# Second float32r part of each weight: ScalarE's negated first part and an adding transfer, in place of VectorE's difference

## The chip, the core and the metric

The kernel runs on one core of one Trainium2 chip. The metric is the device time of one execution in microseconds (us); three runs of the kernel before have a median of 1448.61 us (1447.63 to 1450.83).

## What is computed

One decoder layer on 512 tokens of width 1024, in float32: a SwiGLU feed-forward network (FFN 1), a token mixer that runs gated linear attention (GLA) and softmax attention with forget gates (FoX) side by side and merges them, and a second feed-forward network (FFN 2). Every sub-layer has an RMSNorm before and after it, and shift, scale and gate from a conditioning vector.

```python
h = rmsnorm(x, g_pre[0]) * (1 + sc1) + sh1
x = x + 0.5 * gt1 * rmsnorm(swiglu(h, w_gu1, w_dn1), g_post[0])
h = rmsnorm(x, g_pre[1]) * (1 + sc2) + sh2
x = x + gt2 * rmsnorm(token_mixer(h, ...), g_post[1])
h = rmsnorm(x, g_pre[2]) * (1 + sc3) + sh3
x = x + 0.5 * gt3 * rmsnorm(swiglu(h, w_gu2, w_dn2), g_post[2])
```

All weights are float32: w_gu1 and w_gu2 are 1024 x 5632, w_dn1 and w_dn2 2816 x 1024, w_in 1024 x 8224, w_pa, w_pb and w_out 1024 x 1024, and w_ada, which makes shift, scale and gate, 1024 x 9216.

## The kernel before

**Two parts of every operand.** TensorE takes float32r operands, which have fewer bits than float32. So each weight and each activation is held as two float32r tiles: a first part `hi` (the value rounded) and a second part `lo` (the value minus `hi`). A product is three matmuls, hi by hi, hi by lo and lo by hi (`PARTS`, line 188; `mm3`, line 190). Two of the three read the weight's `hi`, one reads its `lo`.

**Weights come in chunks.** `Block` (line 159) cuts a weight matrix into chunks of 128 x 1024 values (512 KB). `raw_load` (line 147) allocates one of four raw buffers (`NRAW = 4`, tag `raw`) and SyncE issues the load into it. `split` (line 152) allocates one of five `whi` and one of five `wlo` buffers (`NW = 5`); ScalarE copies the raw chunk, rounded, into `whi` (line 155), and VectorE writes raw minus `whi` into `wlo` (line 156). There are 220 chunks; 218 of their differences run on VectorE, two on GpSimd by the argument `eng` (both in the first block, behind the calls of lines 497 and 506). Each chunk feeds 24 matmuls of 512 columns, in whichever stage it is used.

**A ring of buffers.** A raw buffer is free for the next load when both parts have been made; a `whi` or `wlo` buffer is free when the last matmul that reads it is done. `ada_acc` (line 202) loads parts of w_ada into the same four raw buffers, where VectorE multiplies them up (lines 211 and 213), and `two_parts` (line 216) puts the result's two parts into a `wlo` buffer.

**Stages.** The first FFN's first column block is written out by hand, interleaved with the first modulation (from line 444 on, its order fixed by `in_order`). `ffn` (line 381) then runs eleven blocks of gate and up columns, four chunks each, and `down` (line 408) the second matrix in two halves of the output columns, one chunk for two rows of 128, except the last six rows of the second half. Beside the first chunks of a first half, `down` calls `mod_gate` (line 279) twice: it loads four raw buffers of w_ada, sums them on VectorE, splits the sum (`two_parts`) and has TensorE add it over the partitions (lines 294 and 295). The mixer stages take their projections as steps of `Fill`, whose loads are asked for four steps ahead (`LOOK = 4`), with FoX and then GLA work between the steps.

**Order.** Outside the parts fixed by hand, a planner orders the instructions of each engine from the program order and its own estimate of when each is ready. Loads are moved ahead as far as buffers allow, and the matmuls of one product can be moved apart. On the chip each engine then runs its list strictly in that order, and waits at an instruction whose inputs are late.

Of the kernel before, what the change touches and what calls it, by code (L numbers as in the profile page):

```python
# [8 lines left out]
F32 = mybir.dt.float32  # L9
# [3 lines left out]
AF = mybir.ActivationFunctionType  # L13
ALU = mybir.AluOpType
# [25 lines left out]
def tile_hybrid_layer(  # L40
# [4 lines left out]
    nc = tc.nc  # L45
# [12 lines left out]
    def nm(s):  # L58
        uid[0] += 1
        return f"{s}_{uid[0]}"  # L60
# [4 lines left out]
    def tmp(shape=(P, 512), dt=F32):  # L65
        return sb.tile(list(shape), dt, tag="t2", bufs=NTMP, name=nm("t2"))
# [17 lines left out]
    @contextmanager  # L84
    def in_order(last):

        start = len(nc.cur_bb.bb.instructions)
        yield
        for i in list(nc.cur_bb.bb.instructions)[start:]:
            if i.engine in last:  # L90
                after_inst(i, last[i.engine])
            last[i.engine] = i
# [44 lines left out]
    def small_columns():  # L137
        rps = aux((P, P))
        nc.tensor.transpose(rps[:, :108], rows[:108, :], ident[:108, :108])
        nc.vector.tensor_copy(cols, rps[:, :108])  # L140
        cth = small(8)
        nc.scalar.activation(cth, cols[:, 96:104], AF.Tanh, scale=0.5)
        nc.vector.scalar_tensor_tensor(csil, cth, 1.0, cols[:, 96:104], ALU.add, ALU.mult)
        nc.vector.tensor_scalar(csil, csil, 0.5, None, ALU.mult)
# [7 lines left out]
    def split(raw, shape, eng=None):  # L152
        hi = sb.tile([P] + list(shape), F32R, tag="whi", bufs=NW, name=nm("whi"))
        lo = sb.tile([P] + list(shape), F32R, tag="wlo", bufs=NW, name=nm("wlo"))
        nc.scalar.copy(hi, raw)  # L155
        (eng or nc.vector).tensor_tensor(lo, raw, hi.bitcast(F32), ALU.subtract)  # L156
        return hi, lo

    class Block:
# [17 lines left out]
        def load(self, a=0, b=None, eng=None):  # L177
            self.fetch(a, b)
            for r, n in self.spans(a, b):
                if self.parts[r] is None:  # L180
                    hi, lo = split(self.raw[r], (n, self.args[4]), eng)
                    for j in range(n):
                        self.parts[r + j] = (hi[:, j, :], lo[:, j, :])
# [13 lines left out]
    def hilo(hi, lo, src, eng=None):  # L197
        nc.scalar.copy(hi, src)  # L198
        (eng or nc.vector).tensor_tensor(lo, src, hi.bitcast(F32), ALU.subtract)  # L199
# [21 lines left out]
    def ada_fetch_first(ch):  # L221

        w2 = w_ada[:, 0:2 * D].rearrange("(k p) (m c) -> p k m c", p=P, m=2)
        us = []
        for k in range(KD):
            u = unit()
            nc.sync.dma_start(u.rearrange("p (m c) -> p m c", m=2), w2[:, k, :, ch * 256:(ch + 1) * 256])
            us.append(u)
        return us

    def ada_sum_a(us, ks):

        for k in ks:
            nc.scalar.activation(us[k], us[k], AF.Copy, scale=csil[:, k:k + 1])
            if k:
                nc.gpsimd.tensor_tensor(us[0], us[0], us[k], ALU.add)

    def ada_sum_b(us, k0):

        a = tmp()  # L240
        nc.vector.tensor_scalar(a, us[k0], csil[:, k0:k0 + 1], None, ALU.mult)
        for k in range(k0 + 1, KD):
            nc.vector.scalar_tensor_tensor(a, us[k], csil[:, k:k + 1], a, ALU.mult, ALU.add)
        nc.vector.tensor_tensor(a, a, us[0], ALU.add)
        return a
# [19 lines left out]
    def mod_reduce(a):  # L265
        ps = aux((P, 4))
        for j in range(4):
            nc.tensor.matmul(ps[:, j:j + 1], a[:, j * P:(j + 1) * P], ones[:, 0:1], start=True, stop=True)  # L268
        return ps

    def mod_turn(shc, scc, i, ch, ps):
        js = slice(2 * ch, 2 * ch + 2)
        b0 = 24 * i + 2 * ch
        g0 = 72 + 8 * i + 2 * ch
        nc.vector.scalar_tensor_tensor(scc[:, js], ps[:, 2:4], 1.0, cols[:, b0 + 8:b0 + 10], ALU.add, ALU.add)
        nc.vector.tensor_tensor(shc[:, js], ps[:, 0:2], cols[:, b0:b0 + 2], ALU.add)
        nc.vector.tensor_tensor(scc[:, js], scc[:, js], cols[:, g0:g0 + 2], ALU.mult)
# [41 lines left out]
    def x_stat(t):  # L319
        ss = small(2)  # L320
        for h in range(2):
            sumsq(xt[t][h], ss[:, h:h + 1])
        return rstd_of(ss[:, 0:1], ss[:, 1:2], D)
# [9 lines left out]
    def x_turned(tp, xn, dp, bank=aux):  # L333

        ps = bank((P, 2, 256))
        for j in range(2):
            d = 2 * dp + j
            for e in range(2):
                nc.tensor.transpose(ps[:, j, e * P:(e + 1) * P], xn[e][d // 4][:, (d % 4) * P:(d % 4 + 1) * P], ident)
        return ps  # L340
# [27 lines left out]
    def gu_blocks(w_gu, jb):  # L368
        return Block(w_gu, 0, KD, jb * 256, 256), Block(w_gu, 0, KD, DFF + jb * 256, 256)

    def gu_matmuls(ps, gw, uw, hs, ks, ts, js=range(4), late=False):

        for j in js:
            cs = slice(j // 2 * P, (j // 2 + 1) * P)
            p_, w_ = ps[j // 2][j % 2], (gw, uw)[j % 2]
            for n, (k, i, e) in enumerate([(k, *ie) for k in ks for ie in PARTS] if not late else
                                          [(k, *ie) for ie in ((0, 0), (1, 0), (0, 1)) for k in ks]):
                nc.tensor.matmul(p_[:, ts], w_[k][i][:, cs], hs[k][e][:, ts],  # L378
                                 start=ks[0] == 0 and n == 0, stop=ks[-1] == KD - 1 and n == 3 * len(ks) - 1)
# [61 lines left out]
    first = gu_blocks(w_gu1[0], 0)  # L441
    ps0 = [[acc(), acc()] for _ in range(2)]
    last = {}
    with in_order(last):
        ada = []
        for ch in range(4):
            ada.append(ada_fetch_first(ch))
            if ch % 2 == 0:
                for b in first:
                    b.fetch(2 * ch, 2 * ch + 4)  # L450
        rs_ = []
        xn = []

        def norm(t):

            xx = sb.tile([P, D], F32, tag="wlo", bufs=NW, name=nm("xn"))
            for h in range(2):
                nc.vector.tensor_scalar(xx[:, h * 512:(h + 1) * 512], xt[t][h], rs_[t], None, ALU.mult)
            xn.append([xx[:, 0:512], xx[:, 512:1024]])

        for t in range(NT):
            rs_.append(x_stat(t))
            if t == 1:
                norm(0)
                small_columns()

        def turn(tp, dp, eng):
            ps = x_turned(tp, xn[2 * tp:2 * tp + 2], dp, (aux, acc)[dp % 2])
            for j in range(2):
                eng(xT[2 * dp + j][:, tp * 256:(tp + 1) * 256], ps[:, j])  # L470

        def modulated(ch, a, n):

            mod_turn(sh1, sc1, 0, ch, mod_reduce(a))
            ht = [tmp() for _ in range(2)]
            for e in range(2):
                d = 2 * ch + e
                nc.vector.tensor_scalar(ht[e], xT[d], sc1[:, d:d + 1], sh1[:, d:d + 1], ALU.mult, ALU.add)
            if ch < 3:
                ada_sum_a(ada[ch + 1], range(n))  # L480
            for e in range(2):
                d = 2 * ch + e
                hilo(hs[d][0], hs[d][1], ht[e])
            if ch < 3:
                ada_sum_a(ada[ch + 1], range(n, ROWS_A[ch + 1]))

        norm(1)
        norm(2)
        for dp in range(4):
            turn(0, dp, nc.vector.tensor_copy)  # L490
            if dp == 0:
                norm(3)
        ada_sum_a(ada[0], range(ROWS_A[0]))
        for dp in range(4):
            turn(1, dp, nc.scalar.copy)
        a = ada_sum_b(ada[0], ROWS_A[0])
        first[0].load(0, 4)
        first[1].load(0, 4, nc.gpsimd)
        modulated(0, a, 3)
        for ch in range(4):  # L500
            ks, part = (2 * ch, 2 * ch + 1), 3 if ch < 3 else 4
            gu_matmuls(ps0, *first, hs, ks, slice(0, 512), range(part), True)
            if ch < 3:
                a = ada_sum_b(ada[ch + 1], ROWS_A[ch + 1])
                if ch == 1:
                    first[0].load(4, 8)
                    first[1].load(4, 8, nc.gpsimd)
                modulated(ch + 1, a, (5, 4, 0)[ch])
            gu_matmuls(ps0, *first, hs, ks, slice(0, 512), range(part, 4), True)
# [647 lines left out]
```

## Time and profile before

| | before |
|---|---|
| median of 3 runs | 1448.61 us |
| profiled execution | 1448.71 us |
| its span, first to last instruction | 1447.0 us |
| TensorE (PE) busy | 1398.0 us, 97% |
| VectorE (DVE) busy | 764.7 us, 53% |
| ScalarE (ACT) busy | 531.6 us, 37% |
| GpSimd (POOL) busy | 207.3 us, 14% |
| mean busy share of the 16 DMA engines | 39% |
| mean granted TensorE clock | 0.996 |

Stages by the span's time: first block and first modulation to about 65 us, FFN 1's gate and up blocks to about 293, its second matrix to about 430, mixer to about 1062, FFN 2 to the end, with its second matrix from about 1315. In the rows, an engine's name with a q (SPq) is the queue of the engine; "xN" is a number of instructions; in a timeline the bracket tells how long the engine sat idle ahead of the row and what ended that wait. Matmuls overlap in the rows: what counts is the distance between their starts.

### The profile page before, as it was taken

The page shows a single profiled execution, that of the slowest core. Times are in us where ns is not written, and L with a number is a line of the kernel's source. Part 1 is how long each engine was busy: PE and PEld are TensorE (multiplying, and loading weights), DVE is VectorE, ACT ScalarE, POOL GpSimd, SP SyncE. Part 2 cuts the span into 40 slices and gives each one's busy share as a digit, 9 for nine tenths or more (in the row PEclk, how much of TensorE's full clock was granted, in tenths as well). Part 3 has the DMA queues.
Part 4 walks back from the last instruction along what each step waited for, and adds up shares of the span by engine and source line. Part 5 has one row for each costly group of instructions (what it writes and reads, how often), then busy time and mean ns, then how long its engine had stood idle before and what let it go on. Part 6 is the DMA issues. An engine that isn't in the chain of part 4 may idle for free.

```text
span 1447.0 us, 17080 instructions
## 1 busy us (share of the span) xinstructions
PE 1398.0 (97%) x6477; PEld 1123.6 (78%) x6477; DVE 764.7 (53%) x1210; ACT 531.6 (37%) x915; POOL 207.3 (14%) x328
## 2 busy tenths in 40 slices
PE   5899999999999999999999999999999999999998
PEld 4688888878877877777888887788888888887886
DVE  6945544272266689762645546538464434337232
ACT  6332322232244376663733334332353322222221
POOL 6200000000041544340110212100050000000001
PEclk9999999999999999999999999999999999999999
DMA  9544543272335755322332222126613233235411
GB/s 322 158 147 146 155 150 101 60 247 93 96 120 161 227 160 175 95 69 79 97 109 73 73 73 59 59 72 182 197 45 117 87 102 99 91 87 188 132 59 59
DMA packets 160623, 174.40 MB, mean 121 GB/s; under 512 B 8842, under 2 KB 127734, under 8 KB 160540
## 3 DMA queue, kind: packets, MB, share of 16 engines
q1 hardware_dynamic: 160540, 173.31, 39.1%
q8 instruction: 51, 0.84, 0.2%
q14 instruction: 32, 0.26, 0.1%
HBM read 169.05 MB, written 4.23 MB: 120 GB/s over the span
## 4 chain that ended last, share of the span: by engine, by line
PE 83%; DVE 9%; ACT 2%; issue 2%; POOL 1%; DMA 1%; SPq 0%; DVEq 0%; POOLq 0%; ACTq 0%
PE mm L192 44%; PE mm L378 33%; DVE wlo L156 1%; PE aux L980 1%; DVE t L213 1%; PE mm L802 1%; DMA raw<-in_w_dn_dram 1%; PE aux L791 1%; DVE u L779 1%; ACT jk L314 1%; PE aux L268 1%; POOL sm L310 1%; ACT u L775 0%; DVE u L199 0%; DVE u L766 0%
## 5 line engine op out<-in xcount | busy, mean ns | idle before, releaser
L156 DVE TENSOR_TENSOR wlo<-raw,whi 128x1024 fp32r<-128x1024 f32 x218 | 272.3, 1252 | 404.4 <-ACT whi L155 395.2
L378 PE MATMUL mm<-u,whi 128*128 128x512 f32 (+1 forms) x1472 | 451.8, 390 | 10.1 <-ACT u L198 9.7
L155 ACT CAST whi<-raw 128x1024 fp32r<-128x1024 f32 x220 | 230.1, 1050 | 542.3 <-PE mm L192 300.1
L192 PE MATMUL mm<-whi,u 128*128 128x512 f32 x1216 | 390.2, 397 | 1.5 <-ACT u L198 1.5
L378 PEld LDWEIGHTS mm<-u,whi 128*128 128x128 f32 x1472 | 274.7, 190 | 75.4 <-ACT u L198 12.9
L192 PE MATMUL mm<-u,whi 128*128 128x512 f32 x896 | 289.3, 401 | 0.8 <-DVE u L1007 0.8
L378 PE MATMUL mm<-u,wlo 128*128 128x512 f32 (+1 forms) x736 | 283.1, 388 | 0.0
L192 PEld LDWEIGHTS mm<-whi,u 128*128 128x128 f32 x1216 | 228.2, 188 | 54.2 <-ACT u L198 1.7
L192 PE MATMUL mm<-wlo,u 128*128 128x512 f32 x608 | 240.2, 395 | 0.0
L192 PEld LDWEIGHTS mm<-u,whi 128*128 128x128 f32 x896 | 166.9, 189 | 39.2 <-DVE u L1007 1.2
L192 PE MATMUL mm<-u,wlo 128*128 128x512 f32 x448 | 178.4, 399 | 0.0
L378 PEld LDWEIGHTS mm<-u,wlo 128*128 128x128 f32 x736 | 139.6, 190 | 30.9
L192 PEld LDWEIGHTS mm<-wlo,u 128*128 128x128 f32 x608 | 114.2, 188 | 28.0
L192 PEld LDWEIGHTS mm<-u,wlo 128*128 128x128 f32 x448 | 84.7, 189 | 19.6
L307 POOL TENSOR_SCALAR sm<-ss 128x1 f32<-128x1 f32 x12 | 2.3, 191 | 667.6 <-ACT jk L314 667.6
L198 ACT CAST u<-t 128x512 fp32r<-128x512 f32 (+1 forms) x84 | 44.5, 537 | 114.0 <-DVE t L401 78.4
L213 DVE SCALAR_TENSOR_TENSOR t<-raw,csil,t 128x512 f32<-128x512 f32 x98 | 74.0, 755 | 3.3 <-DMA raw<-in_w_ada_dram 1.1
L748 POOL TENSOR_SCALAR u<-t,Ft 128x128 f32<-128x128 f32 (+1 forms) x64 | 43.9, 695 | 89.8 <-DMA t<-Fd 77.7
L400 DVE SCALAR_TENSOR_TENSOR t<-t,mm 128x512 f32<-128x512 f32 x44 | 30.1, 684 | 47.0 <-ACT t L399 47.0
L399 ACT ACTIVATE t<-mm 128x512 f32<-128x512 f32 x44 | 26.1, 594 | 63.2 <-PE mm L378 63.2
L401 DVE SCALAR_TENSOR_TENSOR t<-t,mm 128x512 f32<-128x512 f32 x44 | 30.2, 687 | 30.8 <-PE mm L378 29.2
L199 DVE TENSOR_TENSOR u<-t,u 128x512 fp32r<-128x512 f32 x52 | 35.6, 689 | 16.1 <-ACT u L198 15.9
(178 smaller groups left out, 1121.3 us busy)
## 6 DMA issues: line engine op xcount, KB each, us to landing
raw<-in_w_gu_dram SPq DMA_DIRECT2D x88, 512.0 KB, 4.0
raw<-in_w_in_dram SPq DMA_DIRECT2D x64, 512.0 KB, 3.8
raw<-in_w_dn_dram SPq DMA_DIRECT2D x44, 512.0 KB, 3.7
raw<-in_w_ada_dram SPq DMA_DIRECT2D x64, 256.0 KB, 3.1
raw<-in_w_ada_dram SPq DMA_DIRECT2D x24, 512.0 KB, 3.9
u<-in_w_ada_dram SPq DMA_DIRECT2D x32, 256.0 KB, 6.5
raw<-in_w_in_dram SPq DMA_DIRECT2D x20, 256.0 KB, 3.1
t<-Fd SPq DMA_DIRECT2D x16, 256.0 KB, 4.7
```

The costliest lines, as they stand in the source:

```text
L155: nc.scalar.copy(hi, raw)
L156: (eng or nc.vector).tensor_tensor(lo, raw, hi.bitcast(F32), ALU.subtract)
L192: nc.tensor.matmul(ps, a[i], b[j], start=first and n == 0, stop=last and n == 2)
L198: nc.scalar.copy(hi, src)
L199: (eng or nc.vector).tensor_tensor(lo, src, hi.bitcast(F32), ALU.subtract)
L213: nc.vector.scalar_tensor_tensor(a, raw[:, j, :], csil[:, k:k + 1], a, ALU.mult, ALU.add)
L268: nc.tensor.matmul(ps[:, j:j + 1], a[:, j * P:(j + 1) * P], ones[:, 0:1], start=True, stop=True)
L378: nc.tensor.matmul(p_[:, ts], w_[k][i][:, cs], hs[k][e][:, ts], start=ks[0] == 0 and n == 0, stop=ks[-1] == KD - 1 and n == 3 * len(ks) - 1)
L399: nc.scalar.activation(th, pg, AF.Tanh, scale=0.5)
L400: nc.vector.scalar_tensor_tensor(th, th, 1.0, pg, ALU.add, ALU.mult)
L401: nc.vector.scalar_tensor_tensor(th, th, 0.5, pu, ALU.mult, ALU.mult)
L748: nc.gpsimd.tensor_scalar(s_at(s, i), fb[:, 0:n], -1.0, Ft[:, i, h:h + 1], ALU.mult, ALU.add)
```

## The change

The new code in `split` is used wherever no engine is given. ScalarE runs a second instruction on the raw chunk, a copy with scale -1, into `wlo` (so it holds the first part with its sign turned), and GpSimd issues a transfer that reads the raw chunk and adds it, in float32, to what is in `wlo`. The raw buffer is then free when that transfer has read it, and the matmuls that read `wlo` wait for the transfer. Two calls in the first block now name VectorE and keep the old difference, so 216 of the 220 chunks go the new way, two stay on VectorE and two on GpSimd.

```diff
@@ split @@
         hi = sb.tile([P] + list(shape), F32R, tag="whi", bufs=NW, name=nm("whi"))
         lo = sb.tile([P] + list(shape), F32R, tag="wlo", bufs=NW, name=nm("wlo"))
         nc.scalar.copy(hi, raw)
-        (eng or nc.vector).tensor_tensor(lo, raw, hi.bitcast(F32), ALU.subtract)
+        if eng is None:
+
+            nc.scalar.activation(lo, raw, AF.Copy, scale=-1.0)
+            nc.gpsimd.dma_start(lo.bitcast(F32), raw, accum_op=ALU.add)
+        else:
+            eng.tensor_tensor(lo, raw, hi.bitcast(F32), ALU.subtract)
         return hi, lo
@@ first block @@
-        first[0].load(0, 4)
+        first[0].load(0, 4, nc.vector)
         first[1].load(0, 4, nc.gpsimd)
...
-                    first[0].load(4, 8)
+                    first[0].load(4, 8, nc.vector)
                     first[1].load(4, 8, nc.gpsimd)
```

## Rows read from the trace of the kernel before

**Rows 1.** The page: busy time of the engines, and the DMA queue of the loads.

```profile
PE 1398.0 (97%) x6477; PEld 1123.6 (78%) x6477; DVE 764.7 (53%) x1210; ACT 531.6 (37%) x915; POOL 207.3 (14%) x328
q1 hardware_dynamic: 160540, 173.31, 39.1%
```

**Rows 2.** The page's costliest groups, the two instructions of `split`: busy, mean ns, idle before.

```profile
L156 DVE TENSOR_TENSOR wlo<-raw,whi 128x1024 fp32r<-128x1024 f32 x218 | 272.3, 1252 | 404.4 <-ACT whi L155 395.2
L155 ACT CAST whi<-raw 128x1024 fp32r<-128x1024 f32 x220 | 230.1, 1050 | 542.3 <-PE mm L192 300.1
```

**Rows 3.** Timeline of ScalarE, then of VectorE, in FFN 1's second matrix.

```profile
323.85 1.05 ACT L155 CAST whi<-raw 128x1024 fp32r<-128x1024 f32 x1 [4.60 <-PE mm L192]
329.41 1.05 ACT L155 CAST whi<-raw 128x1024 fp32r<-128x1024 f32 x1 [4.51 <-PE mm L192]
...
324.93 1.23 DVE L156 TENSOR_TENSOR wlo<-raw,whi 128x1024 fp32r<-128x1024 f32 x1 [4.42 <-ACT whi L155]
```

**Rows 4.** Waits of SyncE's queue, in total, times, longest.

```profile
SPq L149 <- DVE wlo L156: 751.9, 154, 15.9
```

**Rows 5.** The page's DMA issues: KB each, median us from issue to landing.

```profile
raw<-in_w_dn_dram SPq DMA_DIRECT2D x44, 512.0 KB, 3.7
```

**Rows 6.** Groups by shape: two of GpSimd's instructions.

```profile
L236 POOL TENSOR_TENSOR u<-u,u 128x512 f32<-128x512 f32 x14 | 20.9, 1499 | 2.7 <-DMA u<-in_w_ada_dram 1.7 <-ACT u L234 0.3
L310 POOL TENSOR_TENSOR sm<-sm,mhalf 128x1 f32<-128x1 f32 x24 | 14.0, 584 | 2.0
```

**Rows 7.** Stretches: us, busy PE, PEld, DVE, ACT, POOL, PEclk, DMA share, GB/s.

```profile
110.00:290.00 180.00, 180.00 (x782) 145.26 (x782) 83.79 (x111) 48.16 (x60) 0.00 (x0) 1.00 0.41 123
290.00:330.00 40.00, 38.69 (x166) 30.82 (x166) 27.19 (x34) 12.09 (x14) 0.00 (x0) 1.00 0.70 237
330.00:420.00 90.00, 89.84 (x390) 72.18 (x388) 28.37 (x31) 24.65 (x41) 6.48 (x17) 1.00 0.30 97
1062.00:1320.00 258.00, 256.92 (x1198) 210.54 (x1199) 111.89 (x140) 76.93 (x110) 15.33 (x22) 1.00 0.31 94
1320.00:1345.00 25.00, 23.82 (x103) 18.87 (x102) 18.32 (x22) 7.84 (x9) 0.00 (x0) 1.00 0.85 285
```

**Rows 8.** Timeline where FFN 1's second matrix starts: SyncE, ScalarE, VectorE.

```profile
299.49 2.15 SPq L289 DMA_DIRECT2D raw<-in_w_ada_dram  x2
...
303.01 0.37 SPq L149 DMA_DIRECT2D raw<-in_w_dn_dram  x1
...
294.55 1.04 ACT L155 CAST whi<-raw 128x1024 fp32r<-128x1024 f32 x1
297.75 1.05 ACT L155 CAST whi<-raw 128x1024 fp32r<-128x1024 f32 x1 [2.15 <-DMA raw<-in_w_dn_dram]
...
307.84 1.05 ACT L155 CAST whi<-raw 128x1024 fp32r<-128x1024 f32 x1 [8.52 <-DMA raw<-in_w_dn_dram]
...
299.99 1.20 DVE L156 TENSOR_TENSOR wlo<-raw,whi 128x1024 fp32r<-128x1024 f32 x1
```

**Rows 9.** Timeline of TensorE in the same stretch.

```profile
298.47 1.33 PE L192 MATMUL mm<-whi,u 128*128 128x512 f32 x5
...
311.84 0.51 PE L294 MATMUL aux<-pair,ones 128*128 128x512 f32 x1 [1.31 <-ACT pair L198]
```

**Rows 10.** Timeline where FFN 1 leaves its first block: ScalarE, then VectorE.

```profile
59.02 2.00 ACT L155 CAST whi<-raw 128x1024 fp32r<-128x1024 f32 x2
...
60.10 2.36 DVE L156 TENSOR_TENSOR wlo<-raw,whi 128x1024 fp32r<-128x1024 f32 x2 [0.18 <-ACT whi L155]
```

**Rows 11.** The page's chain that ended last, by line; then a piece of it in FoX.

```profile
PE mm L192 44%; PE mm L378 33%; DVE wlo L156 1%; PE aux L980 1%; DVE t L213 1%; PE mm L802 1%; DMA raw<-in_w_dn_dram 1%; PE aux L791 1%; DVE u L779 1%; ACT jk L314 1%; PE aux L268 1%; POOL sm L310 1%; ACT u L775 0%; DVE u L199 0%; DVE u L766 0%
...
507.10 1.66 DVE wlo L156
```

**Rows 12.** Timeline of TensorE just behind that piece.

```profile
510.70 0.30 PE L762 MATMUL mm<-u,u 128*128 128x128 f32 x1 [1.31 <-DVE u L630]
```

**Rows 13.** Waits of the engines: one of GpSimd's, in total, times, longest.

```profile
POOL u L748 <- DMA t<-Fd: 77.7, 8, 34.9
```

## The prediction

> **What bounds the kernel now.** I read the busy times first. TensorE is busy 97% of the span, every other engine 53% or less [rows 1], so the end moves only where TensorE comes to wait, or stops waiting. The change touches no matmul. It takes a VectorE instruction out of the making of each weight chunk and puts a longer path in its place, so the question is how early a chunk is ready now. In FFN 1's second matrix ScalarE starts a first part every 5.56 us, each time after a wait for TensorE, that is, for one of the five `whi` buffers [rows 3]. One chunk's 24 matmuls thus take 5.6 us, 0.23 us each. A chunk begun when the fifth chunk ahead of it is done is needed four chunks later, after 4 x 5.6 = 22.4 us. Its second part is ready at 324.93 + 1.23 = 326.16, 2.3 us after 323.85 [rows 3], so it lies ready for 20 us. VectorE's difference is therefore hidden wherever the weights run ahead. It is not hidden where they have just begun to run: at the start of a second matrix [rows 8, 9] and at FFN 1's second column block [rows 10]. Last I read the DMA stretches [rows 7], because the change puts new work there.
>
> **VectorE loses** 216 x 1.252 us = 270 us [rows 2], from 765 to 494 us, off the path in most places. In the chain that ended last the difference stands with 1% of the span, 14 us [rows 11]. One of its pieces, 1.66 us in FoX, has a TensorE wait of 1.31 us for VectorE behind it [rows 11, 12]. What comes free there meets the next point.
>
> **ScalarE gains** 216 x 1.050 us = 227 us, taking the rounding copy as the row for the negated one [rows 2]: from 532 to 758 us, 52%. Each comes ahead of what ScalarE has queued next, in FoX the exponentials. At a place where VectorE gives 1.2 us back ScalarE takes 1.05. I put the whole middle at 0, with 6 us to either side (a gain above the 1.31 us [rows 12] at four or five such places, 14 us [rows 11] being all that the chain holds; a loss of the same count times 1.05).
>
> **GpSimd gains** 216 issues, an operation that the trace doesn't show from GpSimd. Bounds: SyncE's issue, 0.37 us [rows 8], and GpSimd's 512-column sum, 1.50 us [rows 6]. I take the row of GpSimd that moves next to nothing, 0.58 us [rows 6], as an issue moves no data itself: 126 us, from 14% to 23%. Behind a waiting issue stand GpSimd's norm and score instructions, which have room.
>
> **The adding transfer** isn't in the trace either. A load of 512 KB lands 3.7 us after its issue [rows 5]. In the stretch 330 to 420 the DMA engines were busy 0.30 x 90 = 27 us for 97 GB/s x 90 us = 8.73 MB, 16.65 chunks [rows 7]: 1.62 us of all engines for one chunk, and 2.1 us of the landing time for the rest. The adding transfer reads raw, reads `wlo` and writes `wlo`: between one pass (1.62) and three (4.86). I take two, 3.24 us, since the loads too read and write at once for their one pass. It then lands 2.1 + 3.24 = 5.3 us after its issue (3.7 to 7.0). The Trainium skill (Collectives: The Full Stack, "The bandwidth ceiling: the fold count and why AG ≠ RS ≠ AR") says that an add in the DMA engines costs two source reads for each chunk and nothing for the sum itself, which is my two passes; no run here shows it yet. Against that, its page DMA: Bandwidth & Descriptors ("Anatomy of one DMA — SWDGE (gpsimd) path") fits a transfer from GpSimd by 2.0 us and 436 GB/s, an estimate of 3.2 us here; by that the sum below would come to about 1455.
>
> **Second part, from the end of the first.** Before: 326.16 - 324.90 = 1.26 us [rows 3]. After: 1.05 + 0.58 + 5.3 = 6.93 us (5.1 to 9.6). It is 5.7 us later (3.9 to 8.3). Of the 20 us of lead 14 are left, 12 in the worse bound: in steady work this costs nothing, and the lead of three chunks is the cover.
>
> **The raw ring.** A raw buffer is now kept until the transfer is done, 5.7 us longer. SyncE's queue already waits 752 us for second parts ahead of weight loads [rows 4]. With the lead that too is free, except at the starts.
>
> **Start of a second matrix (two places).** At 301.2 VectorE ends a second part (299.99 + 1.20), and only then does SyncE issue the second of the two w_ada loads of its row (the row ends at 301.64); the next weight loads stand behind it, the first at 303.01 [rows 8]. After: the first part ends at 297.75 + 1.05 = 298.8, its second part at 305.7, 4.5 us later; the next weight load goes at 306.1, not 303.0, 3.1 us later, and the next first part starts at 310.9, not 307.84. The gate's sum is as late by 4.5 us, less two differences of 1.2 us that VectorE no longer does in between: its matmul, which already makes TensorE wait 1.31 us [rows 9], goes 2.1 us later, at 313.9. The 16 matmuls on the chunk's first part then run to 317.6; its second part is ready at 310.9 + 1.05 + 6.93 = 318.9: 1.3 us more. And the DMA engines are crowded: 0.70 x 40 = 28 us of loads plus 7 chunks (40 / 5.6) x 3.24 = 23 us make 51 us of work in 40, at FFN 2's 0.85 x 25 = 21 plus 4.5 x 3.24 = 15 make 36 in 25 [rows 7]. One load or adding transfer ahead in the line is 1.62 to 3.24 us; I add 2.5. Together 2.1 + 1.3 + 2.5 = 6 us, twice: **12 us** (0 to 24: none if the planner runs the first-part matmuls of several chunks ahead, as it does for five at 298.47 [rows 9]; 24 with the slower bounds).
>
> **First weights of FFN 1's second column block, and of FFN 2.** Two first parts from 59.02, two second parts by 62.46 [rows 10], needed from about 65. After: first parts end at 60.05 and 62.1, second parts come at 67.0 and 69.1. With the 2 x 16 first-part matmuls ahead (7.4 us) nothing waits, without it 2 us. I take 1 us each, **2 us** (0 to 8).
>
> **Sum.** 1448.7 (the profiled execution, 0.1 us above the median; its span with 1.7 us around it) + 12 + 2 + 0 = **1462.7 us, told as 1462**.
>
> **Rivals.** (1) The DMA engines run full. Now 39.1% x 1447 = 566 us [rows 1]; with 216 x 3.24 = 700 us, 87%. In 110 to 290 us, 0.41 x 180 = 74 us and 32 chunks x 3.24 = 104 make 178 of 180 [rows 7]: my own value lies at the edge, and above 3.3 us a transfer it decides. At 3.9 us this stretch is 19 us too long, and the starts take some 8 more than in my sum: 1490. At 4.86 the stretch needs 230 us (50 more), 1062 to 1320 needs 80 + 46 x 4.86 = 304 for 258 (46 more): about 1560. For it: two reads and a write are a bulk that the loads don't have. Against it: the rows written are 4 KB, the loads' half that or less. (2) VectorE's relief wins: the middle gives its full 6 us and first-part matmuls cover the starts: 1443. It decides if the starts cost under 3 us. For it: rows 11 and 12, and the five matmuls run ahead. Against it: ScalarE takes back nearly the same in the same place. (3) All of it hidden, both terms near zero: 1449. (4) A transfer stuck in GpSimd's queue behind an instruction that waits; GpSimd waits up to 34.9 us for one load [rows 13], more than the lead of 20. One such place costs up to 15 us: 1470 with a second of half that beside my smaller terms. Against it: the planner places both by when they are ready.
>
> **How the numbers follow.** Forecast 0.45; full DMA engines 0.20; relief 0.13; hidden 0.15; stuck queue 0.07. A difference of 0.2% (2.9 us) is about what a measurement of this kernel can tell from none. Slower: 0.45 + 0.20 + 0.07, less 0.02 for small terms in the forecast: 0.70. Same: 0.15 + 0.02 = 0.17. Faster: 0.13. The likeliest case alone reaches from 1449 to 1480; the range takes in the relief at the low end and most of the full-engine case at the high one: 1443 to 1520.
>
> **What would show it.** Right: TensorE waits of several us at about 312 and 1334, in front of `wlo` matmuls, released by a DMA; none between 120 and 290; ScalarE near 758 us; DMA share near 85%; VectorE near 495. The step on the transfer is wrong if it lands under 4 or over 7 us after its issue, the one on GpSimd if an issue is busy over 1.5 us. The whole fails if TensorE waits through FFN 1's blocks (rival 1), or if FoX alone loses more than the starts (ScalarE).

## The result, and the profile after

The changed kernel takes 1534.61 us (median of four executions, 1527.62 to 1537.60) against 1449.72 us beside it (1447.63 to 1451.00): 1.058 times the time, interval 1.0539 to 1.0621. It is slower, by 85 us, where 14 were forecast. The time lies outside the predicted range. The profiled execution took 1527.62 us, span 1525.9 us: 78.9 us more than before.

The page of the changed kernel (engines: busy us, share, instructions; queues: packets, MB, share of 16 DMA engines; groups: busy us, mean ns, idle before; issues: KB, us to landing). Lines behind `split` stand 5 further down in the changed kernel than before.

```profile
PE 1425.6 (93%) x6477; PEld 1140.9 (75%) x6477; DVE 544.6 (36%) x994; ACT 732.2 (48%) x1131; POOL 373.3 (24%) x544
...
q0 software_dynamic: 31104, 113.26, 39.9%
q1 hardware_dynamic: 160540, 173.31, 35.7%
...
L159 POOL DMA_DIRECT2D wlo<-raw x216 | 186.6, 866 | 1050.4 <-ACT wlo L158 828.1
...
wlo<-raw POOLq DMA_DIRECT2D x216, 512.0 KB, 5.3
```

Two readings. First, the transfer itself is about what it was taken for: it lands 5.3 us after its issue, and its queue fills 39.9% of 1525.9 us, 609 us for 216 transfers or 2.82 us each of all DMA engines. Second, the page splits the loss. TensorE has the same 6477 matmuls but is busy 1425.6 us, not 1398.0 [rows 1]: 27.6 us more. The rest of the span, in which it does nothing, grew from 49.0 to 100.3 us: 51.3 us more. So a third of the 78.9 us is matmuls that ran slower, and two thirds are waits.

Where the waits are shows in TensorE's timeline (start us, us, engine, line, operation, idle time before it and what ended it), picked from five places:

```profile
309.79 0.80 PE L197 MATMUL mm<-wlo,u 128*128 128x512 f32 x1 [5.00 <-DMA wlo<-raw]
320.00 0.50 PE L299 MATMUL aux<-pair,ones 128*128 128x512 f32 x1 [0.59 <-ACT pair L203]
326.41 0.50 PE L197 MATMUL mm<-wlo,u 128*128 128x512 f32 x1 [1.45 <-DMA wlo<-raw]
...
449.04 0.66 PE L344 MATMUL aux<-ident,t 128*128 128x128 f32 x2 [4.80 <-DVE t L334]
...
491.23 0.25 PE L724 MATMUL aux<-ident,u 16*128 16x16 f32 x1 [7.75 <-DVE u L717]
...
592.10 0.47 PE L768 MATMUL mm<-u,u 128*128 128x128 f32 x1 [1.96 <-DVE u L637]
...
1394.78 0.80 PE L197 MATMUL mm<-wlo,u 128*128 128x512 f32 x1 [4.97 <-DMA wlo<-raw]
```

The first three and the last are the starts of the two second matrices, where the adding transfer is late. The other three are in the mixer, and there TensorE waits for VectorE, the engine that lost work. What slowed the matmuls shows in the stretches behind such waits (us, busy PE, PEld, DVE, ACT, POOL, the granted clock PEclk, DMA share, GB/s):

```profile
110.00:290.00 180.00, 180.00 (x783) 145.25 (x782) 50.44 (x82) 78.34 (x94) 26.34 (x31) 1.00 0.91 224
...
303.00:310.00 7.00, 2.00 (x8) 1.15 (x7) 3.94 (x6) 2.41 (x3) 1.70 (x2) 0.91 0.90 213
310.00:317.00 7.00, 7.00 (x20) 5.52 (x21) 1.52 (x3) 0.00 (x0) 0.00 (x0) 0.61 1.03 305
317.00:330.00 13.00, 10.96 (x46) 8.13 (x45) 3.56 (x5) 8.32 (x9) 3.40 (x4) 1.00 0.92 219
486.00:500.00 14.00, 8.77 (x21) 6.01 (x22) 6.43 (x11) 1.99 (x2) 0.84 (x1) 0.51 1.04 289
585.00:592.00 7.00, 4.00 (x19) 3.06 (x17) 6.91 (x6) 2.32 (x4) 6.75 (x14) 1.00 0.93 233
592.00:596.00 4.00, 3.90 (x14) 3.64 (x15) 3.30 (x15) 0.00 (x0) 0.00 (x0) 0.57 0.78 243
```

In FFN 1's blocks, 110 to 290 us, TensorE never waits though the DMA engines are busy by 0.91. From 303 to 310 it did 2.00 us of work in 7. Then the granted clock is 0.61 for 7 us (mostly its lower level, 1.2 of 2.4 GHz), and 20 matmuls fill 7.00 us, where 46 fill the next 10.96. The same follows the wait of 7.75 us (0.51) and the one of 1.96 us (0.57), ahead of which TensorE had waited once already: from 585 to 592 it worked 4.00 us of 7. Waits like these are paid for a second time; the short ones of 0.59 and 1.45 us are not (1.00 from 317 to 330). Over the whole run the mean granted clock is 0.976 of 1525.9 us, where it was 0.996 of 1447.0: by my estimate 31 us more of full clock are missing, which is enough for the 27.6 us of busy time.

To place the loss I compare, in the two traces, the start of the n-th of the 6477 matmuls; none is missing. (At some 300 places the two plans order neighbouring matmuls differently, but up to the end of each stretch they hold the same work, all but one matmul.) The table gives how much later it comes, stretch by stretch of the time before. The columns behind the change are experiments, told below; the three that take one part of the layer each add up to the change within 5 us in every stretch.

| stretch (us, time before) | change | FFNs alone | mixer start, FoX alone | GLA, w_out alone | negated copy, VectorE adds |
|---|---|---|---|---|---|
| to 83: first block | 2.2 | 2.6 | 1.4 | 1.3 | 1.4 |
| 83 to 418: FFN 1, start of its second matrix | 11.1 | 13.5 | 0.2 | 0.0 | 0.1 |
| 418 to 446: turn to the mixer | 6.2 | 0.0 | 6.5 | 0.0 | 2.4 |
| 446 to 511: mixer's start, forget gates | 16.4 | 0.2 | 14.5 | 0.0 | 0.1 |
| 511 to 672: FoX pairs | 16.5 | 0.4 | 19.3 | 1.1 | 6.8 |
| 672 to 999: GLA | 2.2 | 0.0 | 0.0 | 2.2 | -0.2 |
| 999 to 1045: w_out | 10.3 | 0.0 | 0.0 | 12.0 | 0.0 |
| 1045 to 1304: start of FFN 2 | 2.7 | 2.6 | -0.1 | -0.1 | 0.9 |
| 1304 to 1440: start of its second matrix | 7.9 | 7.7 | -0.3 | -0.6 | 2.5 |

In the first row 1.3 or so is noise: the kernels that leave the first block as it was (FoX alone, w_out alone) show as much. Another 3.3 us of the change's 78.9 lie behind the last matmul. Between the starts the FFN's blocks lose nothing. The middle, from the turn to w_out, put at 0 in the prediction, loses 51.6 us.

**The turn to the mixer.** In the changed kernel, GpSimd's timeline, then VectorE's:

```profile
435.96 0.95 POOL L655 MEMSET rawg<- 128x1024 f32 x1 [1.20 <-DMA wlo<-raw]
436.87 0.73 POOL L204 TENSOR_TENSOR u<-t,u 128x256 fp32r<-128x256 f32 x1
...
438.09 0.85 POOL L159 DMA_DIRECT2D wlo<-raw  x1
...
439.60 4.43 POOL L204 TENSOR_TENSOR u<-t,u 128x256 fp32r<-128x256 f32 x6
```

```profile
430.75 0.75 DVE L369 SCALAR_TENSOR_TENSOR u<-u,sm,u 128x512 f32<-128x512 f32 x1 [0.43 <-POOL sm L315]
...
438.16 6.43 DVE L369 SCALAR_TENSOR_TENSOR u<-u,sm,u 128x512 f32<-128x512 f32 x1 [0.25 <-POOL sm L315]
```

GpSimd splits the mixer's input (L204), and issues for the mixer's first chunks now stand between these instructions. They run late and in one stretch to 444.0, and VectorE's instruction on the residual, 0.75 us at 430.75, takes 6.43, to 444.6. TensorE's wait of 4.80 us at 449.04 stands behind it. In the kernel before, GpSimd did the same work in one stretch too (422.28 to 428.10), but VectorE's instruction had begun at 422.11 and took 0.74.

**The mixer's start.** VectorE's timeline there:

```profile
478.80 0.49 DVE L216 TENSOR_SCALAR t<-raw,csil 128x512 f32<-128x512 f32 x1 [5.24 <-DMA raw<-in_w_ada_dram]
...
486.10 2.33 DVE L218 SCALAR_TENSOR_TENSOR t<-raw,csil,t 128x512 f32<-128x512 f32 x3 [2.13 <-DMA raw<-in_w_ada_dram]
488.45 0.68 DVE L706 TENSOR_TENSOR u<-u,u 16x512 f32<-16x512 f32 x1
489.17 0.75 DVE L218 SCALAR_TENSOR_TENSOR t<-raw,csil,t 128x512 f32<-128x512 f32 x1
489.95 0.68 DVE L707 SCALAR_TENSOR_TENSOR u<-u,u 16x512 f32<-16x512 f32 x1
490.67 0.41 DVE L717 TENSOR_TENSOR_SCAN u<-ones,u 16x128 f32<-16x128 f32 x1
```

L666 to L717 make the forget gates that FoX begins with. In VectorE's list they are mixed with the multiplications of w_ada (L216, L218), whose loads share the raw ring and come late. Why they are late stands in the waits of SyncE's queue from 430 to 520 us (total, times, longest):

```profile
SPq L149 <- DMA wlo<-raw: 19.1, 4, 15.8
...
SPq L262 <- DMA wlo<-raw: 8.6, 2, 6.6
```

L262 issues the loads of w_ada, L149 those of the weights; both wait for raw buffers that adding transfers have not read yet. In the kernel before, the same two waited 16.1 and 6.7 us for VectorE's second parts (longest 10.2 and 3.6), so these rows alone prove little; the run with a fifth raw buffer, below, tests it.

**The FoX pairs.** GpSimd's timeline of the changed kernel, then VectorE's:

```profile
583.24 0.84 POOL L159 DMA_DIRECT2D wlo<-raw  x1 [8.68 <-ACT wlo L158]
583.82 1.13 POOL L753 TENSOR_SCALAR u<-t,Ft 128x128 f32<-128x128 f32 x2
584.63 1.16 POOL L755 TENSOR_TENSOR u<-u,mneg 128x128 f32<-128x128 f32 x2
585.50 1.51 POOL L753 TENSOR_SCALAR u<-t,Ft 128x384 f32<-128x384 f32 x2
...
590.64 1.11 POOL L755 TENSOR_TENSOR u<-u,mneg 128x128 f32<-128x128 f32 x2
```

```profile
585.04 0.68 DVE L635 SCALAR_TENSOR_TENSOR u<-mm,u 64x512 fp32r<-64x512 f32 x1
585.65 2.59 DVE L637 CAST u<-u 64x512 fp32r<-64x512 f32 x1
...
589.61 2.43 DVE L637 CAST u<-u 64x512 fp32r<-64x512 f32 x1
```

The preparation of a pair's scores (L753, L755) stands behind an issue that waits 8.68 us for ScalarE's negated copy. Released, it runs without a gap from 583.8 to 591.8, just when VectorE makes the key parts: the copy of L637, 0.42 us before, takes 2.59 and 2.43, and TensorE waits for the second.

### The profile page after: what moved, and what is told of

The parts are those of the page before. It is cut to its first block, busy times and chain, and to the rows that moved or that the text cites. A ratio compares the mean times of both kernels' runs of the same rounds, so it can differ in the third digit from the quotient of the medians.

```text
span 1525.9 us, 17533 instructions
## 1 busy us (share of the span) xinstructions
PE 1425.6 (93%) x6477; PEld 1140.9 (75%) x6477; DVE 544.6 (36%) x994; ACT 732.2 (48%) x1131; POOL 373.3 (24%) x544
## 3 DMA queue, kind: packets, MB, share of 16 engines
q0 software_dynamic: 31104, 113.26, 39.9%
## 4 chain that ended last, share of the span: by engine, by line
PE 46%; issue 5%; DMA 5%; DVE 3%; POOL 2%; ACT 2%; POOLq 0%; DVEq 0%; ACTq 0%; SPq 0%
PE mm L197 27%; PE mm L383 16%; DMA raw<-in_w_out_dram 2%; DMA wlo<-raw 2%; PE aux L985 1%; DMA raw<-in_w_dn_dram 1%; POOL u L753 1%; DVE u L637 1%; POOL u L755 1%; ACT u L780 1%; DMA raw<-in_w_ada_dram 0%; PE mm L807 0%; PE aux L796 0%; POOL sm L315 0%; ACT jk L319 0%
## 5 line engine op out<-in xcount | busy, mean ns | idle before, releaser
L159 POOL DMA_DIRECT2D wlo<-raw x216 | 186.6, 866 | 1050.4 <-ACT wlo L158 828.1
L197 PE MATMUL mm<-whi,u 128*128 128x512 f32 x1216 | 400.0, 406 | 6.1 <-ACT jk L319 4.5
L155 ACT CAST whi<-raw 128x1024 fp32r<-128x1024 f32 x220 | 229.5, 1045 | 315.4 <-issue 78.5
L158 ACT ACTIVATE wlo<-raw 128x1024 fp32r<-128x1024 f32 x216 | 227.9, 1057 | 150.5 <-PE mm L197 100.6
L197 PEld LDWEIGHTS mm<-whi,u 128*128 128x128 f32 x1216 | 234.6, 193 | 62.3 <-ACT jk L319 5.0
L197 PE MATMUL mm<-wlo,u 128*128 128x512 f32 x608 | 246.7, 406 | 14.1 <-DMA wlo<-raw 14.1
L197 PEld LDWEIGHTS mm<-wlo,u 128*128 128x128 f32 x608 | 118.0, 194 | 44.0 <-DMA wlo<-raw 16.0
L405 DVE SCALAR_TENSOR_TENSOR t<-t,mm 128x512 f32<-128x512 f32 x44 | 30.2, 687 | 246.6 <-ACT t L404 246.6
L197 PEld LDWEIGHTS mm<-u,wlo 128*128 128x128 f32 x448 | 85.6, 191 | 20.3
L218 DVE SCALAR_TENSOR_TENSOR t<-raw,csil,t 128x512 f32<-128x512 f32 x98 | 73.5, 750 | 42.3 <-DMA raw<-in_w_ada_dram 40.3
L204 DVE TENSOR_TENSOR u<-t,u 128x512 fp32r<-128x512 f32 x52 | 35.7, 692 | 55.6 <-ACT u L203 55.4
L367 DVE TENSOR_TENSOR t<-mm,u 128x512 f32<-128x512 f32 x12 | 8.2, 686 | 117.1 <-ACT jk L319 117.1
L780 ACT ACTIVATE u<-u,sm 128x128 f32<-128x128 f32 (+1 forms) x64 | 35.4, 562 | 28.4 <-DVE sm L778 28.3
L753 POOL TENSOR_SCALAR u<-t,Ft 128x128 f32<-128x128 f32 (+1 forms) x64 | 46.3, 912 | 0.0
```

Source lines behind the costliest of these rows:

```text
L158: nc.scalar.activation(lo, raw, AF.Copy, scale=-1.0)
L159: nc.gpsimd.dma_start(lo.bitcast(F32), raw, accum_op=ALU.add)
L197: nc.tensor.matmul(ps, a[i], b[j], start=first and n == 0, stop=last and n == 2)
L218: nc.vector.scalar_tensor_tensor(a, raw[:, j, :], csil[:, k:k + 1], a, ALU.mult, ALU.add)
L405: nc.vector.scalar_tensor_tensor(th, th, 1.0, pg, ALU.add, ALU.mult)
L753: nc.gpsimd.tensor_scalar(s_at(s, i), fb[:, 0:n], -1.0, Ft[:, i, h:h + 1], ALU.mult, ALU.add)
```

## The experiments

### The change in one part of the layer at a time, and ScalarE's part alone

The flag `xfer[0]` is set anew as the program reaches each part.

```diff
+    xfer = [True]
...
-        if eng is None:
+        if eng is None and xfer[0]:
             nc.scalar.activation(lo, raw, AF.Copy, scale=-1.0)
             nc.gpsimd.dma_start(lo.bitcast(F32), raw, accum_op=ALU.add)
         else:
-            eng.tensor_tensor(lo, raw, hi.bitcast(F32), ALU.subtract)
+            (eng or nc.vector).tensor_tensor(lo, raw, hi.bitcast(F32), ALU.subtract)
```

> The negated copy and the adding transfer are kept in the two FFN layers alone; from the mixer's first weight to its last one (w_out) VectorE subtracts as before. Theory A (the loss has two parts that add up: about 24 us at the starts of the four FFN matrices, where the first chunks come late, and about 50 us in the mixer, where work on VectorE and GpSimd stands behind or beside the transfers): 1473 to 1480 us, the steady stretches at 0. Rival B (the loss is one of DMA load or of ScalarE's extra copies, so it goes with the count of chunks: FFN1 and FFN2 hold 132 of the 216): some 1449 + 85 x 132/216 = 1501 us.

> The new way only from the mixer's first weight to the end of the FoX pairs (50 to 60 of the 216 chunks); VectorE subtracts elsewhere. Theory A: the forget-gate chain and the FoX pairs lose what they lose in the changed kernel, 33 to 39 us, 1482 to 1488 us. Rival B (by the count of chunks): 1449 + 85 x 55/216 = 1471 us.

> The new way only from the end of the FoX pairs through GLA, w_pa and w_out. Theory A: GLA loses 2 us and w_out's start 10, 1459 to 1463 us; there the half-clock spells go with w_out's start. If the three parts add up to the whole change (+85), nothing is passed from one stage to the next. Rival B: by the count of chunks 1449 + 85 x 45/216 = 1467 us.

Measured: 1474.15 us (ratio 1.0170, 1.0152 to 1.0189), 1493.96 us (1.0317, 1.0296 to 1.0338) and 1463.45 us (1.0099, 1.0082 to 1.0116), beside 1448.65 us before. The losses are 25.5, 45.3 and 14.8 us; they add up to 85.6, and the whole change lost 84.9. So, within the few us by which the table's columns differ from the change, no stage hands its loss on to the next. The transfers number 128, 32 and 56 (instructions of GpSimd beyond the 328 of before), not quite as the expectations had counted them; by these counts rival B would be 1499, 1461 and 1471 us. It fails in the first two: 32 transfers cost over half of the loss, 128 less than a third. Theory A's places hold; FoX's part was put some 6 us too low, perhaps because it was taken from the changed kernel's one profile, its fastest run.

```diff
             nc.scalar.activation(lo, raw, AF.Copy, scale=-1.0)
-            nc.gpsimd.dma_start(lo.bitcast(F32), raw, accum_op=ALU.add)
+            nc.vector.tensor_tensor(lo, raw, lo.bitcast(F32), ALU.add)
```

> Everywhere ScalarE makes the negated copy, but VectorE adds the raw buffer to it in place of the transfer: ScalarE's load is that of the changed kernel, there is no transfer and no issue on GpSimd. Theory A (ScalarE's extra copies have room; the loss comes of the transfer and of what waits in GpSimd's queue): 1449 to 1458 us. Rival C (ScalarE's 228 us of extra copies set the loss, through a later second part): over 1490 us.

Measured: 1461.00 us (ratio 1.0082, 1.0067 to 1.0098), 3 us above theory A's band and far under rival C. ScalarE's load is there in full; VectorE keeps its work, which now also waits for the negated copy. TensorE's waits in the pairs, 500 to 690 us, are nearly all of one kind. The page's engines and the longest entry of those waits, of this kernel:

```profile
PE 1402.7 (96%) x6477; PEld 1125.3 (77%) x6477; DVE 770.0 (53%) x1210; ACT 733.8 (50%) x1131; POOL 206.1 (14%) x328
```

```profile
PE mm L767 <- DVE u L635: 7.7, 6, 2.1
```

In the kernel before, the same wait came to 4.0 us. The making of the key and query parts goes to and fro between ScalarE and VectorE, and a negated copy of 1.06 us can stand ahead of it. That is worth 6.8 us in the pairs by the table, and 12 us in all: a term of its own, a seventh of the loss.

### The FoX pairs: queue, copy, ring

All start from the FoX-only kernel (1494 us). In the first, from the first pair on, the issue is pinned behind what was written ahead of it on GpSimd:

```diff
-            nc.gpsimd.dma_start(lo.bitcast(F32), raw, accum_op=ALU.add)
+            i = nc.gpsimd.dma_start(lo.bitcast(F32), raw, accum_op=ALU.add)
+            if pinned[0]:
+                tc.keep_in_program_order(i)
```

> As xfer_fox (1494 us), but from the first FoX pair on each transfer is issued behind the score preparation that was written ahead of it: the preparation no longer stands behind an issue that waits for ScalarE. Theory Q (GpSimd's queue holds the preparation back, and it then runs in one burst beside VectorE's copies for the next pair, which take 2.2 us in place of 0.4): the copies return to about 0.5 us, the FoX pairs lose 3 to 10 us in place of 19, 1478 to 1485 us; the loss ahead of the pairs (21 us) stays. Rival L (the later second part itself holds TensorE up): 1494 us or more, as the issues come no earlier.

Measured: 1485.74 us (ratio 1.0255, 1.0238 to 1.0272), 1 us above theory Q's band. In the second, the copy is ScalarE's:

```diff
-                    nc.vector.tensor_copy(kx[e][o], ky[e][n])
+                    nc.scalar.copy(kx[e][o], ky[e][n])
```

> As xfer_fox (1494 us), but the copy of a key half from one half of the partitions to the other, which took 2.2 us on VectorE where GpSimd worked beside it, is made by ScalarE; GpSimd's queue is as it was. Theory Q: the slow copies go, the FoX pairs lose 5 to 12 us in place of 19, 1480 to 1488 us. Rival L: no change, 1492 to 1498 us. Rival C (ScalarE is the engine that is short): slower still, over 1498 us.

Measured: 1478.74 us (ratio 1.0199, 1.0183 to 1.0216), 1 us below theory Q's band. In the third:

```diff
-NU = 69
+NU = 67
-NRAW = 4
+NRAW = 5
```

> As xfer_fox (1494 us), with five raw buffers in place of four and 67 unit tiles in place of 69. Theory R (a raw buffer is held until the transfer has read it, so the gate's weights, which use the same ring, are loaded late and VectorE stands before them with the forget-gate chain behind): the 11 to 15 us at the mixer's start fall to 0 to 5, 1480 to 1486 us. Rival D (the DMA engines are crowded there): 1490 to 1496 us.

Measured: 1477.22 us (ratio 1.0190, 1.0175 to 1.0205), 3 us below theory R's band. By the same matmuls as above, in us later than before:

| stretch | FoX only | issue pinned | copy on ScalarE | five raw buffers |
|---|---|---|---|---|
| 418 to 446 | 6.5 | 6.8 | 6.4 | 3.3 |
| 446 to 511 | 14.5 | 17.5 | 12.3 | 6.5 |
| 511 to 555, first pairs | 7.0 | 7.8 | 6.4 | 8.4 |
| 555 to 672, other pairs | 12.3 | 1.9 | 2.1 | 7.8 |

The two edits that share nothing but the copy's neighbourhood, one moving GpSimd's work and one moving the copy, take the same 10 us out of the same stretch, and nothing elsewhere beyond 3 us to either side. That settles the mechanism there: theory Q holds, rivals L and C fail. The copy by itself (duration ns min/median/max, of FoX), in the kernel before, in the changed one together with L633, its neighbour that reads PSUM (the memory that TensorE writes its results to) and one tile of SBUF (the memory of all the other tiles), and with the issue pinned:

```profile
L632 DVE CAST u<-u x16: 410/416/980, 492.5 to 630.7; 64x512 fp32r<-64x512 f32 x16
```

```profile
L637 DVE CAST u<-u x16: 420/1348/2875, 526.0 to 682.5; 64x512 fp32r<-64x512 f32 x16
L633 DVE TENSOR_TENSOR u<-mm,u x16: 667/688/695, 525.3 to 681.1; 64x512 fp32r<-64x512 f32 x16
```

```profile
L644 DVE CAST u<-u x16: 416/459/2645, 515.0 to 663.5; 64x512 fp32r<-64x512 f32 x16
```

Of these two only the instruction that reads and writes SBUF alone is slowed; L633 keeps its 0.69 us beside the same GpSimd work. The Trainium skill (SBUF — State Buffer, "Who interferes with whom") says that copies and casts of VectorE can take a port pair that GpSimd also uses, and that the loser stands still; an instruction with at most one SBUF input, outside those forms, does not contend. The rows agree, with up to 2.9 us for 0.42; that every overlap blocks they don't show: at 565.67 us the same copy took 0.44 with GpSimd at work.

The fifth raw buffer takes 11 us out of the two stretches ahead of the pairs and halves the mixer's start: theory R, with 6.5 us left there where it allowed 5, and some of the pairs' loss gone as well. The pin left 8 us in the first pairs, which none of these edits moved; what holds them is not shown by itself.

### A plain copy beside VectorE's difference

```diff
         (eng or nc.vector).tensor_tensor(lo, raw, hi.bitcast(F32), ALU.subtract)
+        if eng is None:
+            nc.scalar.dma_start(scr[nscr[0]], raw.rearrange("p a b -> p (a b)"))
+            nscr[0] += 1
```

> The kernel before (VectorE subtracts), and beside it every one of these chunks is copied from the raw buffer to a buffer in DRAM that nobody reads, by a transfer that ScalarE issues right after its rounding copy. It leaves out the adding, ScalarE's second copy and GpSimd's issue; raw buffers are held and the DMA engines loaded about as in the change. Theory R: the starts and the mixer's start lose 10 to 25 us together, the FoX pairs nothing, 1459 to 1474 us. Rival Q alone (only GpSimd's queue and the later second part matter): 1449 to 1453 us.

Measured: 1474.22 us (ratio 1.0169, 1.0145 to 1.0193), at the upper end of theory R's band (0.2 us above it) but not in its places: the starts of the second matrices lost nothing (-0.6 and 0.4 us), the mixer's start 7.4, and the pairs 10.7, where nothing was expected. The total proves nothing. Nor is the copy as heavy as the expectation has it: it lands in 2.7 us where the adding transfer takes 5.3, and takes 1.32 us of all DMA engines for 2.82. Raw buffers held and DMA engines loaded by about half cost the starts nothing; for the full size this run does not show it. In the pairs ScalarE now held the issue, and its other work stood behind. The page's queue and issue, and ScalarE's wait in 480 to 700 us:

```profile
q10 hardware_dynamic: 31392, 114.31, 19.5%
...
scr<-raw ACTq DMA_DIRECT2D x218, 512.0 KB, 2.7
```

```profile
ACT u L781 <- DMA raw<-in_w_in_dram: 10.5, 2, 6.3
```

L781 are the exponentials, which read no weight: they stood behind an issue whose raw buffer had not landed. It is the effect seen on GpSimd, on another engine.

### The starts, and what is left when the causes are out

```diff
+                    e = nc.vector if jb == 0 else None
-                    gw.load(kk, kk + 4)
-                    uw.load(kk, kk + 4)
+                    gw.load(kk, kk + 4, e)
+                    uw.load(kk, kk + 4, e)
...
-                wp.load()
+                wp.load(eng=nc.vector if dh == 0 and k0 < 8 else None)
```

> As xfer_ffn (1474 us: the transfer in the FFN layers alone), but VectorE subtracts for the chunks that open a matrix: the first four of each down matrix and of FFN2's first matrix. Theory S (the FFN layers lose only where the first second parts come 5 us later and TensorE's clock halves after the wait; between the starts the transfer costs nothing): 1449 to 1454 us. Rival D (the transfers slow the weight loads wherever they run): 1460 us or more.

Measured: 1453.37 us (ratio 1.0028, 1.0018 to 1.0038), as theory S has it. With the FFN's transfers kept except for the first chunks, 20.8 of the 25.5 us are gone; TensorE's busy time falls from 1409.4 us (FFNs alone) to 1398.5, so 10.9 of them were slow matmuls. Its trace is 5.2 us late at 95 us, 3.3 of it behind the first block, from 83 on, and not later anywhere after that. So the change is free in steady work.

> The change with its three losing places taken out: VectorE subtracts for the chunks that open a matrix and from the mixer's first weight to the first FoX pair; in the FoX pairs the key half is copied by ScalarE. The transfer stays for the rest, some 165 of 216 chunks. If the three causes are all (later first parts at the starts, gate weights behind held raw buffers, VectorE's copies beside GpSimd's burst), 1453 to 1460 us: 2 to 6 in the FoX pairs and 2 to 4 in GLA are left. If something else in the change costs time by the count of chunks, over 1475 us.

Measured: 1467.45 us (ratio 1.0125, 1.0109 to 1.0140), 7 us over the band and 8 under a loss by the count of chunks; 186 transfers are left, more than the 165 expected. By stretches, 83 to 418 loses 1.3, the turn 0.0, the mixer's start -0.3, FFN 2's second matrix -0.3, and the pairs keep 5.5; but 999 to 1045 still loses 7.3, though w_out's first half is VectorE's there. Its VectorE timeline, and the waits of SyncE's queue from 985 to 1060 us:

```profile
1052.34 0.69 DVE L303 SCALAR_TENSOR_TENSOR u<-aux,u 128x512 f32<-128x512 f32 x1 [19.57 <-DMA u<-in_g_post_dram]
```

```profile
SPq L296 <- DMA wlo<-raw: 18.9, 3, 11.1
SPq L149 <- DMA wlo<-raw: 13.9, 4, 4.7
```

The gate's row of g_post is issued behind loads that wait for raw buffers. Hence two more kernels, with five of them:

> As parts_all (1467 us), with five raw buffers and 67 unit tiles. Theory R (what is left at w_out, 7 us, and ahead of the FoX pairs, 3 us, comes of raw buffers that transfers hold: SyncE's queue stands before them, and the gate's row and weights behind it come late): 1456 to 1461 us. Rival D (the transfer's own load, or ScalarE's copies, cost that): 1465 to 1468 us.

> The changed kernel whole (1535 us) with five raw buffers and 67 unit tiles. Theory R: what fox_ring5 won at the transition and at the mixer's start (11 us) is won here too, and half of w_out's 10: 1515 to 1524 us; the starts of the FFN matrices (two of 8 us) and the FoX pairs keep their loss. Rival D: 1530 us or more.

Measured: 1460.46 us (ratio 1.0071, 1.0053 to 1.0088) and 1513.59 us (1.0442, 1.0423 to 1.0461). The first is inside theory R's band: w_out's 7.3 us are gone (0.0), and some 3 come back in GLA. In the second the turn falls from 6.2 to 1.9 and the mixer's start from 16.4 to 6.4; w_out keeps 9.9, the stretches with the second matrices' starts 7.2 and 7.3, and the pairs lose 21.9 where they lost 16.5: 1 us below theory R's band, and in its places but for w_out and the pairs. What holds w_out there shows in TensorE's one long wait, and in VectorE's product with the gate's row:

```profile
1087.50 0.79 PE L197 MATMUL mm<-whi,u 128*128 128x512 f32 x1 [6.86 <-ACT jk L319]
```

```profile
1084.80 1.33 DVE L301 SCALAR_TENSOR_TENSOR u<-aux,u 128x512 f32<-128x512 f32 x2 [25.65 <-DMA u<-in_g_post_dram]
```

ScalarE's sums of squares (L319) stand behind VectorE's products with the gate, and these behind g_post. No wait of TensorE at w_out is for a late second part here; in the changed kernel 1.89 us are, beside 4.53 for the sums. So the gate's row makes the larger part of TensorE's waits at w_out, here as in the kernel with the causes out (4.73 us, the only long one). SyncE issues its second half at 1071.43 us, and VectorE starts 13.4 us later; before, that half landed 6.0 us after its issue. The row thus comes late twice, at its issue and on its way. The DMA engines are full on the way (1.06 from 1068 to 1085), but so they were before (1.03 from 1021 to 1029); which of the two delays weighs more, no run separates.

> The kernel before with five raw buffers and 67 unit tiles. The control of fox_ring5: if the raw ring holds nothing up there without the transfer, 1447 to 1452 us; if the ring itself was short before, 1440 to 1446 us, and then a part of the 17 us that fox_ring5 won over xfer_fox belongs to the kernel before.

> The kernel before with the key half's copy in the FoX pairs on ScalarE in place of VectorE (16 copies of 0.4 to 1.0 us). If that copy beside GpSimd already costs the kernel before something, 1445 to 1449 us; if ScalarE's longer chain costs more, 1450 to 1455 us.

Measured: 1449.42 us (ratio 0.9999, 0.9990 to 1.0008) and 1452.11 us (1.0013, 1.0004 to 1.0022). The ring was not short before; the fifth buffer helps against the transfers alone. Nor is the copy on ScalarE a gain by itself. No version ran faster than the kernel before.

## Why the prediction was wrong

**What held.** The transfer: 5.3 us to landing, as forecast, with some luck in the parts: 2.82 us of the DMA engines for 3.24, and so 2.5 us for 2.1 of the rest; an issue 0.87 us for 0.58, inside its bounds; together a DMA share of 76% for 85. ScalarE is busy 732 us for 758. TensorE waits in front of `wlo` matmuls, released by a DMA, at both second matrices, and nowhere in FFN 1's blocks from 120 to 290. So rival 1, full DMA engines, is out (0.91 in the stretch that the prediction put at 178 of 180 us); so are rivals 2 and 3, relief and all hidden. VectorE is busy 545 us for 495: some of its instructions got longer, most of all L637 beside GpSimd's work (22.9 us in all for 7.9).

**The starts: right mechanism, two terms short.** At FFN 1's second matrix the waits are 5.00, 0.59 and 1.45 us, less the 1.31 of before [rows 9]: 5.7 us, for a forecast of 6. That is luck, since they are spread otherwise: the first second part alone makes 5.00 for 1.3, the gate less than before. ScalarE's timeline there, in the changed kernel:

```profile
298.85 1.05 ACT L155 CAST whi<-raw 128x1024 fp32r<-128x1024 f32 x1
301.94 1.05 ACT L155 CAST whi<-raw 128x1024 fp32r<-128x1024 f32 x1 [2.04 <-DMA raw<-in_w_dn_dram]
...
303.41 2.00 ACT L158 ACTIVATE wlo<-raw 128x1024 fp32r<-128x1024 f32 x2
```

The first chunk's first part ends at 299.90, but its negated copy starts at 303.41: in ScalarE's list it stands behind the next chunk's rounding copy, which waits for its load. So TensorE has the second part 9.9 us after the first, at 309.79; the sum 1.05 + 0.58 + 5.3 = 6.93 had no term for these 3.5 us. (The same order, with 3.3 us, stands at FFN 2's second matrix.)

And the stretch lost 11.1, of which 2.1 by 95 us, behind the first block, and 9.1 here. What the waits leave of that is mostly the clock: 303 to 317 us shows it fall at the wait, and from 310 to 317 a matmul takes 0.35 us, behind that 0.24. The prediction had no term for that anywhere. Over the whole kernel it is 27.6 us of the 78.9, TensorE's gain in busy time. With FFN 2's and the first block's part the FFN layers lose 25.5 us for 14.

**The middle: the step that failed.** "I put the whole middle at 0, with 6 us to either side" weighed only VectorE's 1.25 us against ScalarE's 1.05; the middle lost 51.6. ScalarE's part is indeed about that size (6.8 us in the pairs, VectorE adding). Three other steps failed in it.

- "Behind a waiting issue stand GpSimd's norm and score instructions, which have room." They have room in time, but it matters when they run: delayed, the split of the mixer's input and the score preparation meet instructions of VectorE that then take longer (6.43 us for 0.75, 2.59 for 0.42). In the pairs, pinning the issue or moving the copy gave back 10 us; at the turn no run tests it alone. Rival 4 had the queue the wrong way round: a transfer stuck behind GpSimd's work, where it is GpSimd's work that is stuck behind a transfer's issue. For each instruction that a change lets wait, one should read which engine's instructions the delayed ones will then run beside.
- "With the lead that too is free, except at the starts" was said of the raw ring. It is true of weights, which run ahead. The ring also serves the gates' w_ada, with no such lead, and SyncE's queue in order; VectorE stands before these loads with the forget gates behind. Five buffers in place of four give back 21 us of the change's 85 (1534.61 to 1513.59).
- "Two places" for the start of a second matrix: w_out is a third, by the same `down` and the same gate. It cost 10.3 us, more by the gate's late row (4.53 us of wait) than by a late second part (1.89).

The condition "if FoX alone loses more than the starts (ScalarE)" depends on what FoX is: the pairs lose 16.5 us beside 19 in the stretches of the two second matrices, but with the mixer's start it is 33, and the FoX-only kernel lost 45.3 us where the FFNs alone lost 25.5. By the wider reading it was met, though ScalarE is not the reason: its copies cost 12 us everywhere together. Left open: some 3 to 8 us in the first pairs, 6.5 at the mixer's start with five buffers, why the pairs then lose 5 more in the whole change, 2 us in GLA, and 3.3 behind the last matmul.

## What to carry to other kernels

Work taken off an engine that nobody waits for brings nothing, and what replaces it has to be followed through every list it joins: whoever stands behind a waiting issue, whoever shares the buffer that is now held longer, and whoever the delayed work then meets. Hidden in steady work is not hidden at starts: keep the short path for the first chunks of each matrix, count every matrix, and look where in its engine's list each step of a longer path will stand. And price a wait of TensorE at more than its length, since the matmuls behind it may run at the lower clock.

## What the runs showed of the hardware

An adding transfer between two SBUF tiles took 2.82 us of all DMA engines for 512 KB; the plain copy of the same chunks to DRAM took 19.5% of 1471.2 us for 218, 1.32 us each. The ratio is 2.1. The Trainium skill (Collectives: The Full Stack, "The bandwidth ceiling: the fold count and why AG ≠ RS ≠ AR") has two source reads for an add; the ratio fits that, and no run here counts the reads. Its time by the fit of DMA: Bandwidth & Descriptors ("Anatomy of one DMA — SWDGE (gpsimd) path"), an estimate of 3.2 us, does not agree with the 5.3 measured. And two short waits in a row, 1.13 and 1.96 us with 4.00 us of work in the 7 from 585 to 592, were followed by a stretch at a granted clock of 0.57.
